# Seven products for one more pair in the output projection, its operand in eight forms, and the second weight sum written over the raw page

## The chip, the cores and the metric

The kernel runs on one core of a Trainium2 chip. The metric is the device time of one execution in microseconds (us). Engines are named as the profile names them: PE (TensorE matmuls), PEld (its weight loads), DVE (VectorE), ACT (ScalarE), POOL (GpSimd) and SP (SyncE, which here only issues DMAs).

## The reference, cut to what matters

Two layers, each with two large products; the change touches how both are computed, the second one most:

```python
for l in range(DEPTH):                      # 2 layers, SEQ = 256, D_MODEL = 4096
    h = rmsnorm(x, norm_w[l])
    proj = h @ w_in[l]                      # 4096 x 11264
    ...                                     # grouped attention and two-way retention on parts of proj
    x = x + jnp.concatenate([a_out, r_out], axis=-1) @ w_out[l]   # 4096 x 4096
return rmsnorm(x, final_norm)
```

All is in float32, so each product of the reference is made from high and low parts.

## The kernel before, in words

**Stages and blocks.** There are four stages: w_in and w_out of layer 0, then of layer 1. A w_in stage has 11 blocks, a w_out stage 4; a block makes 1,024 columns of the output for all 256 rows. Within a block the 4,096 rows of the weight are taken as 16 pairs of 128 + 128 rows. The activations are the stationary operand; the weights stream, 512 columns at a time.

**High and low parts.** A weight page arrives raw from HBM on SP's queue (`wraw`, 128x1024 float32, 512 KB). ACT rounds it to a high part (`whi`), DVE subtracts to get the low part (`wlo`). Operands are split in the same way. Each product is three matmuls of 128x512: high by high, high by low (both at line 1683), and low by high (line 1693).

**Eight products or seven.** A pair is a 2x2 by 2x2 block product. Plainly it takes eight products: two raw pages, 24 matmuls, operand `x8h`/`x8l` of four forms. The pairs in `SEVENS` (2, 5, 8, 9, 11, 13, in every stage) take seven products in Winograd's form: 21 matmuls, operand `x7h`/`x7l` of seven forms (A11, A12, S4, A22, S1, S2, S3). Their weights come as page A (raw), page T (`wv`: ACT copies the raw page, and a DMA from POOL's queue adds a second matrix to it, line 729), half a page B (`third`, 256 KB, split into `bhi`/`blo`) and page U (`wu`: two DVE sums of `wraw`, `wv` and `third`).

**Buffers.** There are 6 raw pages, 5 `whi`, 4 `wlo`, 2 `wv`, one `wu`. `Weights.begin` handles a page. At page T of a seven it makes the two sums into `wu` and calls `empty`, which frees the raw page and issues the next raw load. An eight's raw page is freed after its low part.

**What sets the order.** Nothing is scheduled on the chip: while the program is being written, a planner (`tick`, `room`, `low_parts`, `add_up`) keeps estimated clocks of ACT and DVE and decides where in each engine's fixed order a cast, a sum, a combine or a task of attention stands. Its constants are set per block by `assume(n)` from `PLANS`; `LOW_AHEAD` says how far ahead of PE's clock DVE may be given low parts.

**First blocks and block ends.** The first block of a stage (`opening`) takes its pairs in `FIRST_ORDER`, since its operands are only then being split (`split_pair`). At a block's end the last pair's products are sorted by PSUM bank, and `combine` adds the banks M1 to M8 into two result pages `ca` and `cb`: on DVE from the bank, or through an ACT copy (`out`) when DVE has more than `RELIEF` us queued. The next block starts in banks M3 and M8.

Of the kernel before, what the change touches and what calls it, by code (L numbers as in the profile page):

```python
# [12 lines left out]
F32R = mybir.dt.float32r  # L13
# [4 lines left out]
P = 128  # L18
# [19 lines left out]
A_EARLY = 0  # L38
# [36 lines left out]
SUM_SLACK = 0.3  # L75
# [24 lines left out]
LOW_AHEAD = 1.5  # L100
# [11 lines left out]
    1: {'LOW_AHEAD': 5.0},  # L112
    6: {'TIGHT_A': 8},
    7: {'SUM_SLACK': 0.0, 'AT_ONCE': 1, 'STRICT': 4},
    8: {'TIGHT_B': 5, 'STRICT': 5},
    9: {'THIRD_SLACK': 1.0, 'BANK_REST': 1.5, 'LOW_AHEAD': 1.0, 'RAW_SLACK': 1.0, 'RELIEF': 0.7, 'PASS': 0.1},
    14: {'STRICT': 9, 'TIGHT_A': 0},
    15: {'S_FIXED': 0.16, 'LONG': 2, 'EARLY': 1.8, 'PASS': 0.3, 'PE_REST': 2.0, 'NEAR': 30},
    22: {'PASS': 0.3, 'U_SLACK': 1.0, 'AT_ONCE': 1},
    24: {'V_FIXED': 0.12, 'TIGHT_B': 20, 'TIGHT_A': 2},  # L120
# [12 lines left out]
EIGHTS = [_p for _p in range(NP) if _p not in EVER]  # L133

# [110 lines left out]
LEADS = [8 * next(_i for _i, _p in enumerate(_o) if _p in SEVENS[_s]) for _s, _o in enumerate(FIRST_ORDER)]  # L245
# [91 lines left out]
def hybrid_encoder(  # L337
# [143 lines left out]
    class Weights:  # L481


        def __init__(self):
            self.pages, self.sevens = [], []
            for l in range(DEPTH):
                for w, twice, n in ((w_in, twice_in, N_IN), (w_out, twice_out, N_OUT2)):
                    for b in range(n):
                        stage = 2 * l + (w is w_out)
                        start = (l, b) == (0, 0) and w is w_in  # L490
                        for g in GROUPS[stage] if b else FIRST_GROUPS[stage]:
                            for slot in slots_of(g, stage, start):
# [3 lines left out]
                                one.seven = one.pair in SEVENS[stage] and not one.whole  # L496
# [139 lines left out]
        def begin(self, g):  # L636
# [12 lines left out]
            elif g.kind == PAGE_T:  # L649
# [4 lines left out]
                u = o.u = t(wp, [P, 2, NB], "wu", 1)  # L654
# [4 lines left out]
                self.empty(next(v for v in self.seq if v.own is o))  # L659
# [94 lines left out]
    def dead_room():  # L754

        if not rooms:
            e, o = len(EIGHTS), len(EVER)
# [6 lines left out]
            for p in range(NP):  # L764
                if p not in EIGHTS:
# [22 lines left out]

    def split_pair(p, v, whole, stage):
# [15 lines left out]
        if p in SEVENS[stage]:  # L805
# [20 lines left out]
            ve.tensor_sub(lo[:, 2:7, :], f, f32(hi)[:, 2:7, :])  # L826
            sums_of.pop()
            drop()
        else:
# [3 lines left out]
            else:  # L833
                both = [t(ap, [P, 7, P], v, len(EVER), F32R) for v in ("x7h", "x7l")]
                hi, lo = (v[:, 0:4, :].rearrange("p (i m) t -> p i (m t)", m=MT) for v in both)
# [1260 lines left out]
```

## Time and profile before

| | |
|---|---|
| median of 3 runs | 2599.41 us (2598.05 to 2601.19) |
| the profiled execution | 2599.34 us, its span 2597.6 us |
| PE busy | 2581.8 us, 99% of the span, 11,560 matmuls |
| PEld busy | 2135.2 us, 82% |
| DVE busy | 2215.3 us, 85% |
| ACT busy | 1853.6 us, 71% |
| DMA | 653.5 MB, mean 252 GB/s |
| PE clock | 0.998 of full speed over the span |

Busy time is the union of an engine's instructions. A 128x512 matmul is shown with 0.39 us from start to end, but the next one starts 0.23 us later, so that a pause of PE shows as idle only where it is longer than the overlap of 0.16 us.

### The profile page before, as it was taken

To read this page: it belongs to the slowest core of one execution; us is meant where nothing else is said; L and a number is where in the kernel's file an instruction comes from. 1 tells how busy PE (TensorE), PEld (TensorE's weight loads), DVE (VectorE), ACT (ScalarE), POOL (GpSimd) and SP (SyncE) were. 2 spreads that over 40 slices of the span, in tenths; PEclk is the share of its full clock that TensorE was granted. 3 is DMA by queue.
4 is the path that set the end of the run, shared out by engine and by line. 5 is a ranking of instruction groups with operands and counts; after the bars stand their busy time and mean duration, and the time that the engine had idled before them with its cause. 6 is when DMAs were issued, how large, how long until landed. Compare 5 with 4: busy or idle time off the path is not lost.

```text
span 2597.6 us, 34368 instructions
## 1 busy us (share of the span) xinstructions
PE 2581.8 (99%) x11560; PEld 2135.2 (82%) x11560; DVE 2215.3 (85%) x2710; ACT 1853.6 (71%) x2626; POOL 398.6 (15%) x548
## 2 busy tenths in 40 slices
PE   9999999999999999999999999999999999999998
PEld 7888888888888888888878888888888888888886
DVE  7898888888789898777979888889888798987777
ACT  8877777766666788656887667776666667886655
POOL 0111221221102100211111112221201021000000
PEclk9999999999999999999999999999999999999999
DMA  9988988888778778988888879888887787788886
GB/s 314 305 237 277 289 242 254 281 247 263 221 220 260 230 235 227 271 269 248 275 253 261 250 239 279 246 270 268 259 257 222 208 259 242 220 229 251 250 243 194
DMA packets 206594, 653.52 MB, mean 252 GB/s; under 512 B 24784, under 2 KB 31440, under 8 KB 206416
## 3 DMA queue, kind: packets, MB, share of 16 engines
q1 hardware_dynamic: 147040, 472.99, 51.8%
q0 software_dynamic: 58656, 177.24, 30.7%
q8 instruction: 90, 1.47, 0.2%
q10 hardware_dynamic: 720, 1.10, 0.1%
q14 instruction: 88, 0.72, 0.1%
HBM read 607.19 MB, written 44.04 MB: 251 GB/s over the span
## 4 chain that ended last, share of the span: by engine, by line
PE 94%; DMA 2%; DVE 2%; ACT 1%; issue 1%; SPq 0%; DVEq 0%; POOLq 0%; POOL 0%; ACTq 0%
PE M L1683 60%; PE M L1693 30%; PE M L1158 1%; PE M L1157 1%; PE M L1156 1%; DMA ca<-in_x 1%; DVE wlo L321 1%; ACT whi L321 1%; DMA third<-in_w_out 0%; PE M L1677 0%; DMA wraw<-in_w_out 0%; DVE cb L321 0%; DMA whole<-in_w_in 0%; ACT ca L321 0%; DVE ca L321 0%
## 5 line engine op out<-in xcount | busy, mean ns | idle before, releaser
L321 DVE TENSOR_TENSOR wlo<-wraw,whi 128x1024 fp32r<-128x1024 f32 (+1 forms) x774 | 935.3, 1215 | 172.8 <-issue 61.2
L321 ACT CAST whi<-wraw 128x1024 fp32r<-128x1024 f32 (+1 forms) x776 | 800.1, 1045 | 297.1 <-PE M L1683 283.0
L1683 PE MATMUL M<-whi,x8h 128*128 128x512 f32 x2368 | 922.5, 390 | 1.0 <-DVE cb L321 0.8
L1683 PE MATMUL M<-whi,x8l 128*128 128x512 f32 x2368 | 921.8, 389 | 0.0
L1693 PE MATMUL M<-wlo,x8h 128*128 128x512 f32 x2364 | 676.3, 389 | 0.2 <-DVE wlo L321 0.2
L1683 PEld LDWEIGHTS M<-whi,x8h 128*128 128x128 f32 x2368 | 444.6, 188 | 94.9 <-DVE cb L321 1.5
L1683 PEld LDWEIGHTS M<-whi,x8l 128*128 128x128 f32 x2368 | 444.6, 188 | 92.4 <-DVE x8l L321 0.3
L1693 PEld LDWEIGHTS M<-wlo,x8h 128*128 128x128 f32 x2364 | 442.2, 188 | 91.4 <-DVE wlo L321 1.0
L1683 PE MATMUL M<-whi,x7h 128*128 128x512 f32 x1080 | 420.5, 389 | 0.2 <-ACT whi L321 0.2
L1683 PE MATMUL M<-whi,x7l 128*128 128x512 f32 x1080 | 420.3, 389 | 0.0
L1693 PE MATMUL M<-wlo,x7h 128*128 128x512 f32 x1080 | 334.4, 390 | 0.7 <-DVE wlo L321 0.6
L729 POOL DMA_DIRECT2D wv<-in_twice_in x132 | 118.5, 898 | 1068.6 <-ACT wv L321 923.8
L321 ACT CAST whi<-wu 128x1024 fp32r<-128x1024 f32 x180 | 189.3, 1052 | 91.9 <-DVE wu L321 54.2
L321 ACT CAST whi<-wv 128x1024 fp32r<-128x1024 f32 x180 | 189.0, 1050 | 91.5 <-PE M L1683 51.9
L321 DVE TENSOR_TENSOR wlo<-wv,whi 128x1024 fp32r<-128x1024 f32 x180 | 219.6, 1220 | 37.3 <-PE M L1693 30.7
L321 ACT COPY wv<-wraw 128x1024 f32<-128x1024 f32 x180 | 188.9, 1049 | 74.7 <-DMA wraw<-in_w_out 35.2
L321 DVE TENSOR_TENSOR wlo<-wu,whi 128x1024 fp32r<-128x1024 f32 x180 | 219.1, 1217 | 24.8 <-PE M L1693 16.7
L1693 PEld LDWEIGHTS M<-wlo,x7h 128*128 128x128 f32 x1080 | 202.4, 188 | 44.1 <-DVE wlo L321 2.5
L1683 PEld LDWEIGHTS M<-whi,x7h 128*128 128x128 f32 x1080 | 202.8, 188 | 42.6 <-ACT whi L321 0.9
L1683 PEld LDWEIGHTS M<-whi,x7l 128*128 128x128 f32 x1080 | 202.8, 188 | 41.8
L321 DVE TENSOR_TENSOR wu<-wu,third 128x512 f32<-128x512 f32 x180 | 124.6, 692 | 7.0 <-DMA third<-in_w_in 0.8
L321 DVE TENSOR_TENSOR wu<-wraw,wv 128x512 f32<-128x512 f32 x180 | 123.1, 684 | 8.7 <-DMA wv<-in_twice_in 6.3
(249 smaller groups left out, 2292.0 us busy)
## 6 DMA issues: line engine op xcount, KB each, us to landing
wraw<-in_w_in SPq DMA_DIRECT2D x568, 512.0 KB, 5.2
wraw<-in_w_out SPq DMA_DIRECT2D x208, 512.0 KB, 5.4
wv<-in_twice_in POOLq DMA_DIRECT2D x132, 512.0 KB, 7.5
third<-in_w_in SPq DMA_DIRECT2D x132, 256.0 KB, 5.8
wv<-in_twice_out POOLq DMA_DIRECT2D x48, 512.0 KB, 8.1
third<-in_w_out SPq DMA_DIRECT2D x48, 256.0 KB, 5.7
full<-next_dram POOLq DMA_DIRECT2D x18, 512.0 KB, 9.5
p_dram<-room POOLq DMA_DIRECT2D x64, 128.0 KB, 3.4
```

The costliest lines, as they stand in the source:

```text
L321: return call(out, *args, **kwargs)
L729: self.adds.pop(0)[1]()
L1156: nc.tensor.matmul(out, a[0], b[0], start=start, stop=False)
L1157: nc.tensor.matmul(out, a[0], b[1], start=False, stop=False)
L1158: nc.tensor.matmul(out, a[1], b[0], start=False, stop=stop)
L1683: nc.tensor.matmul(acc[name], a[i], g.hi[h], start=m == first[name] and not i, stop=False)
L1693: nc.tensor.matmul(acc[name], a, g.lo[h], start=False, stop=m == final[name])
```

## The change

- Pair 3 joins `SEVENS` in the two w_out stages (`FLEX = (3,)`). In the first block of such a stage it still takes eight products (`OPENING` leaves it out); in the other three blocks seven.
- Its operand has eight forms (`xfh`/`xfl`, 128x8x128): the seven of before and A21, so that both ways find what they need. In the w_in stages four of them hold the plain operand.
- The second sums are made in place: `u = o.a`, the raw page. `wu` is gone, and the raw page is freed after the low part of page U instead of after the sums.
- `A_EARLY` 1 moves the load of each seven's raw page one place earlier; `SUM_SLACK` is 0.0, `LOW_AHEAD` 3.0; `PLANS` and three of the four `SPREAD`s have other values.

```diff
-A_EARLY = 0
+A_EARLY = 1
-SUM_SLACK = 0.3
+SUM_SLACK = 0.0
-LOW_AHEAD = 1.5
+LOW_AHEAD = 3.0
 PLANS = {
...
-    15: {'S_FIXED': 0.16, 'LONG': 2, 'EARLY': 1.8, 'PASS': 0.3, 'PE_REST': 2.0, 'NEAR': 30},
+    15: {'AT_ONCE': 2, 'SUM_SLACK': 0.0, 'V_FIXED': 0.14, 'PE_REST': 1.5, 'U_SLACK': 0.3, 'RUSH': 2.0},
...
-SEVENS = ((2, 5, 8, 9, 11, 13), (2, 5, 8, 9, 11, 13), (2, 5, 8, 9, 11, 13), (2, 5, 8, 9, 11, 13))
+SEVENS = ((2, 5, 8, 9, 11, 13), (2, 3, 5, 8, 9, 11, 13), (2, 5, 8, 9, 11, 13), (2, 3, 5, 8, 9, 11, 13))
+FLEX = (3,)
+OPENING = tuple(tuple(_p for _p in _s if _p not in FLEX) for _s in SEVENS)
...
-SPREAD2 = (2, 3, 6, 7, 10, 13)
+SPREAD2 = (3, 4, 6, 9, 13, 14)
...
-                u = o.u = t(wp, [P, 2, NB], "wu", 1)
+                u = o.u = o.a
                 ve.tensor_add(u[:, 0, :], o.a[:, 1, :], o.v[:, 0, :])
                 ve.tensor_add(u[:, 1, :], u[:, 0, :], o.b)
-                self.empty(next(v for v in self.seq if v.own is o))
...
-                self.parts(g, o.u)
+                self.parts(g, o.u, then=partial(self.empty, next(v for v in self.seq if v.own is o)))
...
+            n = 8 if p in FLEX else 7
+            hi, lo = seven_room(p)
+            f = page([P, n - 2, P], "xf")
             ac.copy(a22, x1[:, 1])
+            if p in FLEX:
+                ac.copy(tokens(f)[:, 5], x1[:, 0])
...
-            ac.copy(hi[:, 2:7, :], f)
+            ac.copy(hi[:, 2:n, :], f)
...
+            elif p in SEVENS[stage]:
+                a = at(operand[p], ALL, {(0, 0): A11, (1, 0): A12, (1, 1): A22, (0, 1): 7}[index], ALL)
```

PE, second w_out block of layer 0, the first of pair 3's two pages, before (`x8h_8540` is pair 3's operand; M1 to M8 are the banks):

```order
L1683 MATMUL M3_9609<-whi_9699,x8h_8540 128x512
L1683 MATMUL M3_9609<-whi_9699,x8l_8541 128x512
L1683 MATMUL M8_9616<-whi_9699,x8h_8540 128x512
L1683 MATMUL M8_9616<-whi_9699,x8l_8541 128x512
L1683 MATMUL M4_9633<-whi_9699,x8h_8540 128x512
L1683 MATMUL M4_9633<-whi_9699,x8l_8541 128x512
L1683 MATMUL M2_9636<-whi_9699,x8h_8540 128x512
L1683 MATMUL M2_9636<-whi_9699,x8l_8541 128x512
L1693 MATMUL M3_9609<-wlo_9719,x8h_8540 128x512
L1693 MATMUL M8_9616<-wlo_9719,x8h_8540 128x512
L1693 MATMUL M4_9633<-wlo_9719,x8h_8540 128x512
L1693 MATMUL M2_9636<-wlo_9719,x8h_8540 128x512
```

The second page has twelve more of the same. Of the change, in the same place, the last two pages of pair 3, B and U (`xfh_8376` is its operand):

```order
L1697 MATMUL M2_9568<-bhi_9667,xfh_8376 128x512
L1697 MATMUL M2_9568<-bhi_9667,xfl_8377 128x512
L1707 MATMUL M2_9568<-blo_9668,xfh_8376 128x512
L1697 MATMUL M6_9670<-whi_9684,xfh_8376 128x512
L1697 MATMUL M6_9670<-whi_9684,xfl_8377 128x512
L1697 MATMUL M4_9565<-whi_9684,xfh_8376 128x512
L1697 MATMUL M4_9565<-whi_9684,xfl_8377 128x512
L1707 MATMUL M6_9670<-wlo_9701,xfh_8376 128x512
L1707 MATMUL M4_9565<-wlo_9701,xfh_8376 128x512
```

Pages A and T have six each, so that pair 3 now has 21 matmuls for 24; over the whole program PE's order has 11,547 rows where it had 11,565.

DVE in the same stretch, before (rows 2 and 4 are the low parts of pair 3's two pages, row 6 the low part of pair 2's page U):

```order
L321 TENSOR_TENSOR wlo_9701<-wraw5_9555,whi_9677 128x1024
L321 TENSOR_TENSOR wlo_9719<-wraw4_9586,whi_9699 128x1024
L321 STREAM_TRANSPOSE room_9711<-ca_9530 128x1024
L321 TENSOR_TENSOR wlo_9747<-wraw3_9614,whi_9715 128x1024
L321 STREAM_TRANSPOSE room_9737<-cb_9531 128x1024
L321 TENSOR_TENSOR wlo_9773<-wu_9661,whi_9742 128x1024
```

And with the change:

```order
L325 TENSOR_TENSOR wlo_9630<-wraw5_9434,whi_9610 128x1024
L325 TENSOR_TENSOR wraw5_9434<-wraw5_9434,wv_9516 128x512
L325 TENSOR_TENSOR wraw5_9434<-wraw5_9434,third_9514 128x512
L325 TENSOR_TENSOR wlo_9646<-wraw3_9478,whi_9628 128x1024
L325 STREAM_TRANSPOSE room_9638<-ca_9459 128x1024
L325 TENSOR_TENSOR wlo_9662<-wv_9516,whi_9644 128x1024
L325 TENSOR_TENSOR wlo_9686<-wraw4_9537,whi_9660 128x1024
L325 TENSOR_TENSOR blo_9668<-third_9514,bhi_9667 128x512
L325 STREAM_TRANSPOSE room_9680<-cb_9460 128x1024
L325 TENSOR_TENSOR wlo_9701<-wraw5_9434,whi_9684 128x1024
```

Pair 3 now has four low parts and two sums on DVE where it had two low parts, and its raw page `wraw5_9434` is held from its first row here to its last.

DVE at the end of the first block of layer 1, before (`M3_11784` and `M8_11791` are that block's banks; `wlo` rows belong to the block that follows):

```order
L321 SCALAR_TENSOR_TENSOR cb_12433<-cb_12433,M5_11903 128x512
L321 TENSOR_TENSOR cb_12433<-cb_12433,M3_11784 128x512
L321 TENSOR_TENSOR wlo_12517<-wraw5_12385,whi_12481 128x1024
L321 TENSOR_TENSOR cb_12433<-cb_12433,M8_11791 128x512
L321 TENSOR_TENSOR ca_12432<-ca_12432,M4_11820 128x512
```

And with the change:

```order
L325 SCALAR_TENSOR_TENSOR cb_12402<-cb_12402,M5_11887 128x512
L325 TENSOR_TENSOR wlo_12444<-wraw5_12281,whi_12416 128x1024
L325 TENSOR_TENSOR cb_12402<-cb_12402,out_12451 128x512
L325 TENSOR_TENSOR cb_12402<-cb_12402,out_12464 128x512
L325 TENSOR_TENSOR ca_12401<-ca_12401,M4_11735 128x512
```

There banks M3 and M8 are now emptied by ACT copies (`out`), and DVE adds the copies instead of the banks; a low part stands ahead of both.

## Rows read from the trace of the kernel before

**Rows 1.** The page: span, and busy time of each engine.

```profile
span 2597.6 us, 34368 instructions
PE 2581.8 (99%) x11560; PEld 2135.2 (82%) x11560; DVE 2215.3 (85%) x2710; ACT 1853.6 (71%) x2626; POOL 398.6 (15%) x548
```

**Rows 2.** Waits of PE: engine, line, releaser: us in total, times, longest.

```profile
PE M L1693 <- DVE wlo L321: 0.8, 2, 0.6
PE M L1683 <- DVE cb L321: 0.8, 1, 0.8
PE M L1683 <- DVE ca L321: 0.2, 1, 0.2
PE M L1683 <- ACT whi L321: 0.2, 1, 0.2
```

**Rows 3.** Busy time in stretches: the last three w_out blocks of each layer.

```profile
core 0: us, PE busy (x) PEld busy (x) DVE busy (x) ACT busy (x) POOL busy (x), PEclk, DMA share, GB/s
1037.00:1285.00 248.00, 248.00 (x1095) 205.33 (x1095) 200.08 (x228) 167.22 (x222) 43.27 (x60) 1.00 0.88 271
2325.00:2572.00 247.00, 246.39 (x1087) 203.63 (x1086) 194.07 (x209) 156.06 (x187) 20.91 (x24) 1.00 0.82 241
```

**Rows 4.** Busy time in stretches: the two stretches in which a w_out stage opens.

```profile
900.00:1000.00 100.00, 100.00 (x459) 83.46 (x459) 91.54 (x133) 83.86 (x134) 8.70 (x11) 1.00 0.77 229
2200.00:2300.00 100.00, 100.00 (x458) 83.14 (x457) 91.54 (x130) 85.14 (x136) 10.16 (x11) 1.00 0.77 229
```

**Rows 5.** Timeline of PE, rows with idle time in brackets: start, us, instruction.

```profile
1290.83 0.50 PE L1693 MATMUL M<-wlo,x8h 128*128 128x512 f32 x1 [0.22 <-DVE wlo L321]
...
1298.41 0.50 PE L1683 MATMUL M<-whi,x8h 128*128 128x512 f32 x1 [0.23 <-DVE ca L321]
...
1332.88 0.50 PE L1683 MATMUL M<-whi,x7h 128*128 128x512 f32 x1 [0.17 <-ACT whi L321]
...
1382.15 0.50 PE L1683 MATMUL M<-whi,x8h 128*128 128x512 f32 x1 [0.80 <-DVE cb L321]
...
2571.36 0.50 PE L1693 MATMUL M<-wlo,x7h 128*128 128x512 f32 x1 [0.61 <-DVE wlo L321]
```

**Rows 6.** Timeline of DVE and of ACT at the end of layer 1's first block.

```profile
1380.28 1.22 DVE L321 TENSOR_TENSOR wlo<-wraw,whi 128x1024 fp32r<-128x1024 f32 x1
1381.41 0.68 DVE L321 TENSOR_TENSOR cb<-cb,M 128x512 f32<-128x512 f32 x1
...
1380.03 2.00 ACT L321 CAST whi<-wraw 128x1024 fp32r<-128x1024 f32 x2 [2.06 <-PE M L1683]
```

**Rows 7.** Groups by line and form: xcount | busy us, mean ns | idle before.

```profile
L321 DVE TENSOR_TENSOR wlo<-wraw,whi 128x1024 fp32r<-128x1024 f32 x768 | 931.3, 1219 | 172.8 <-issue 61.2 <-ACT whi L321 51.1 <-PE M L1693 48.4
L321 DVE TENSOR_TENSOR blo<-third,bhi 128x512 fp32r<-128x512 f32 x180 | 123.1, 684 | 0.0
L321 DVE TENSOR_TENSOR wu<-wraw,wv 128x512 f32<-128x512 f32 x180 | 123.1, 684 | 8.7 <-DMA wv<-in_twice_in 6.3
L321 ACT CAST whi<-wraw 128x1024 fp32r<-128x1024 f32 x768 | 795.3, 1050 | 295.4 <-PE M L1683 281.3 <-ACT whi L321 4.6 <-issue 4.6
L321 ACT CAST bhi<-third 128x512 fp32r<-128x512 f32 x180 | 111.2, 618 | 15.1 <-PE M L1683 14.5 <-DMA third<-in_w_in 0.4
L321 DVE TENSOR_TENSOR x7l<-xf,x7h 128x640 fp32r<-128x640 f32 x24 | 19.7, 819 | 3.7 <-ACT x7h L321 3.7
L321 DVE TENSOR_TENSOR x8l<-full,x8h 128x256 fp32r<-128x256 f32 x42 | 15.8, 417 | 0.6 <-ACT x8h L321 0.6
L321 DVE TENSOR_TENSOR xf<-xf,full 128x128 f32<-128x128 f32 x21 | 6.0, 285 | 1.8 <-ACT xf L321 1.5
```

**Rows 8.** Raw pages: SP's waits before their loads, their landing, and one wait of DVE.

```profile
SPq L531 <- DVE wu L321: 606.3, 175, 9.0
...
DMA to landing us min/median/max: 3.0/5.3/14.9
...
DVE wlo L321 <- PE M L1693: 95.8, 122, 1.6
```

More of the change, by code (lines that the diff above doesn't have):

```diff
@@ L216 @@
 ]
-SPREAD = (3, 5, 8, 11, 12, 13)
+SPREAD = (3, 5, 8, 10, 12, 13)
 SPREAD1 = (4, 7, 8, 10, 12, 14)
-SPREAD2 = (2, 3, 6, 7, 10, 13)
-SPREAD3 = (6, 7, 9, 11, 12, 14)
+SPREAD2 = (3, 4, 6, 9, 13, 14)
+SPREAD3 = (5, 7, 9, 12, 13, 14)
 def opening_order(stage):
     spread = (SPREAD, SPREAD1, SPREAD2, SPREAD3)[stage]
-    spread = spread if len(spread) == len(SEVENS[stage]) else SEVENS[stage]
-    order = [_p for _p in ([1, 0] if stage == 0 else [0, 1]) + list(range(2, NP)) if _p not in SEVENS[stage]]
-    for i, p in zip(spread, SEVENS[stage]):
+    spread = spread if len(spread) == len(OPENING[stage]) else OPENING[stage]
+    order = [_p for _p in ([1, 0] if stage == 0 else [0, 1]) + list(range(2, NP)) if _p not in OPENING[stage]]
+    for i, p in zip(spread, OPENING[stage]):
         order.insert(i, p)
@@ L236, in grouped @@
     for p in order:
-        if p in SEVENS[stage] or not groups:
+        if p in OPENING[stage] or not groups:
             groups.append(())
@@ L244, with pages_of @@
 FIRST_GROUPS = [grouped(_o, _i) for _i, _o in enumerate(FIRST_ORDER)]
-LEADS = [8 * next(_i for _i, _p in enumerate(_o) if _p in SEVENS[_s]) for _s, _o in enumerate(FIRST_ORDER)]
+LEADS = [8 * next(_i for _i, _p in enumerate(_o) if _p in OPENING[_s]) for _s, _o in enumerate(FIRST_ORDER)]
 SHARED = ("M1", "M5", "M7", "M6")
-def pages_of(group, stage, first=False):
-    n = 1 if group[0] in SEVENS[stage] else 0
+def pages_of(group, sevens, first=False):
+    n = 1 if group[0] in sevens else 0
     order, one, rest = [], group[:n], group[n:]
@@ L262, in pages_of, with slots_of @@
     return order + rest
-def slots_of(group, stage, first=False):
-    for _p, _k in pages_of(group, stage, first):
-        if _p in SEVENS[stage] and not (first and _p in NATIVE):
+def slots_of(group, sevens, first=False):
+    for _p, _k in pages_of(group, sevens, first):
+        if _p in sevens and not (first and _p in NATIVE):
             yield [(_b, _p, (ALL, _a), _k, _h) for _b, _a, _pg, _h in SEVEN_PRODUCTS if _pg == _k]
@@ L490, in __init__ @@
                         start = (l, b) == (0, 0) and w is w_in
+                        sevens = SEVENS[stage] if b else OPENING[stage]
                         for g in GROUPS[stage] if b else FIRST_GROUPS[stage]:
-                            for slot in slots_of(g, stage, start):
+                            for slot in slots_of(g, sevens, start):
                                 one = Page()
@@ L495, in __init__ @@
                                 one.whole = start and one.pair in NATIVE
-                                one.seven = one.pair in SEVENS[stage] and not one.whole
+                                one.seven = one.pair in sevens and not one.whole
                                 one.begun, one.low_at, one.empty, one.raw_at = False, None, False, 1e9
@@ L833, in split_pair @@
             else:
[L834 to L835 removed]
+                hi, lo = (v[:, 0:4, :].rearrange("p (i m) t -> p i (m t)", m=MT) for v in seven_room(p))
             if whole is None:
@@ L1552, in block @@
         rush[0] = RUSH if hurried else 0.0
+        sevens = OPENING[stage] if opening else SEVENS[stage]
         for g in FIRST_GROUPS[stage] if opening else GROUPS[stage]:
-            for slot in slots_of(g, stage, first_order):
+            for slot in slots_of(g, sevens, first_order):
                 flat += slot
```

32 lines of the change are left out of this document (17 added, 15 removed).

## The prediction, made before the changed kernel was run

> **What bounds the kernel now.** I read the page first: PE is busy for 2581.8 us of a span of 2597.6 us, DVE for 85% and ACT for 71% of it [rows 1]. Busy PE alone proves little, because the records of neighbouring matmuls overlap, so the second view is the count of matmuls in a stretch without pauses: the last three w_out blocks of layer 0 hold 1095 matmuls in 248.00 us, which is 0.2265 us each, at the full granted clock of 1.00 [rows 3]. Those three blocks need 3 x 366 = 1098 matmuls (10 pairs of 24, 6 of 21), so there is no hole in them: PE takes its next matmul as soon as it can, and the time of such a block is its number of matmuls. The third view is what PE waited for: wlo 0.8, cb 0.8, ca 0.2 and whi 0.2 us, 2.0 us in all the steady work [rows 2]. The timeline puts these at five places, four where layer 0 goes over into layer 1 and one near the end [rows 5]. Each hides 0.16 us more under the overlap (0.39 us shown, 0.23 us apart), so these five pauses are worth 0.22 + 0.23 + 0.17 + 0.80 + 0.61 + 5 x 0.16 = 2.83 us. That is all that better order could win here; the rest is matmuls, the start and the tail.
>
> The Trainium skill speaks against this reading. Its page "Perfetto Trace Analysis", section "Identifying the Most-Contended Engine", says that busy time of matmuls is no good measure for TensorE, that the busy share of weight loads should be taken instead, and that the most-contended engine is the one with the highest occupancy. By that PE stands at 82% and DVE at 85%, and DVE would be the bound; the second rival below is what that would mean. The count of matmuls in a stretch disagrees with it here.
>
> **Part by part.** *Removed matmuls.* Pair 3 goes from 24 to 21 matmuls in three w_out blocks of each of two layers: 6 x 3 = 18 fewer, which is also the difference of PE's two orders. On the path, since PE has no hole there: 18 x 0.2265 = 4.08 us less.
>
> *Added casts, low parts and sums.* As eight products, pair 3 needs two low parts on DVE (2 x 1.22 = 2.44 us) and two casts on ACT (2 x 1.05 = 2.10). As seven it needs three whole low parts, a half one and two sums: 3 x 1.22 + 0.68 + 2 x 0.68 = 5.70 us on DVE; and three casts, a half one and a copy, 4 x 1.05 + 0.62 = 4.82 us, on ACT, where I take the copy for a cast of its size [rows 7]. That is 3.26 us of DVE and 2.72 us of ACT more per block, 19.6 and 16.3 us in six blocks. In the stretch of layer 0, DVE works 200 of 248 us and ACT 167; with three such blocks this becomes 210 and 175 of 247, and in layer 1 less [rows 3]. PE stays the fullest by 37 us per three blocks, so I cost it at nothing. What hides it is the lead of DVE over PE: it waited 122 times for PE to give a low page back [rows 8], so all four low pages were full then. If that cover were gone, all 19.6 us would show.
>
> *The operand in eight forms.* In each opening of w_out pair 3's split grows. DVE: from two low parts of 256 (0.83 us) to four sums of 0.29, one low part of 256 and one of 768: 1.14 + 0.42 + 0.82 x 768/640 = 2.54 us, an estimate from those rows; so 1.7 us more per layer [rows 7], and something over 1 us on ACT. The two stretches where this falls show DVE at 91.54 of 100 us and PE without idle [rows 4]: 8.5 us are free for 1.7. Bounds: nothing, or 3.4 us in both layers. I take 0.5 us, near the lower end, because the free time is five times the need, but the work comes in bursts.
>
> *The raw page held longer.* This concerns all 180 sevens. Before, SP waited 175 times for the sums into `wu` (606.3 us) and then issued the next raw load [rows 8]; now that load stands behind the low part of page U, one or more low parts later in DVE's order, and behind the waiting load on SP's queue stand later raw loads and the thirds. In the orders I counted, for each raw load, the matmuls from PE's use of the low part that frees the page (or the one next after the sums) to the first matmul on the new page: never under 58 before; 37 once in nearly every block now, and 19 at one place. 37 matmuls are 37 x 0.2265 = 8.4 us; a landing takes 5.3 us in the middle and the cast 1.05 us [rows 7, 8], 6.4 us, so 2.0 us are left even if DVE had no lead. The worst landing of 14.9 us would not be covered. For the sevens themselves, whose added matrix needs the raw page earliest, `A_EARLY` makes up for it: from the freeing low part to page T's first matmul I count at least 76 matmuls, 72 before. Bounds: nothing, or 0.5 us in each of 30 blocks. I take nothing.
>
> *One stall goes.* The longest wait of PE, 0.80 + 0.16 = 0.96 us at 1382.15, is for bank M8: DVE did a low part of 1.22 us first and added the bank only from 1381.41 to 1382.09, while ACT sat idle for 2.06 us [rows 5, 6]. In the changed order both M3 and M8 are emptied there by ACT copies, which need no turn on DVE. I take 0.96 us off. What is late next is not PE's bank but the added copy, which nobody on PE waits for.
>
> *Other order.* At ten block ends of attention and retention a low part that PE uses 16 matmuls (3.6 us) or more after the bank now stands ahead of M3's add, which was so nowhere before. M3 is wanted 19 matmuls, 4.3 us, after its last product, and M8, with 15, stood behind such a low part before in seven of these ends without an idle row; so nothing, and up to 0.4 us each, 4 us, if DVE comes late. The other four pauses, 2.83 - 0.96 = 1.87 us, I leave as they are: ahead of three of them DVE's two orders carry a like amount of work, and the fourth, ACT's, I can't tell. Added DMA is 256 KB in each of six blocks, 1.5 of 653 MB: nothing.
>
> Sum, against the profiled execution of 2599.34 us: - 4.08 - 0.96 + 0.5 = - 4.54, giving 2594.8 us. The median of the three runs is 2599.41, so the same offset holds: 2594.8 us, 0.18% less.
>
> **Rivals.** *The last pauses close as well.* The change has other numbers for the block that opens layer 1, where four of the five pauses lie. If they all go and the openings cost nothing: 2599.4 - 4.08 - 2.83 = 2592.5 us. For it: that block's order is wholly different. Against it: low parts and combines are as many as before.
>
> *DVE is the bound.* Then the removed matmuls win nothing and the 19.6 + 3.4 = 23.0 us added to DVE show: 2599.4 + 23.0 = 2622 us. For it: 85% over the span, 91.5% in the openings [rows 1, 4]. Against it: not one missing matmul in the last three blocks and DVE itself waiting for PE [rows 3, 8]. This is the result that the rule cited above would give (the Trainium skill, "Perfetto Trace Analysis", "Identifying the Most-Contended Engine").
>
> *Raw pages run short.* The rival on the slower side: with six raw pages, each seven's held until page U's low part is made, the load of the eight that follows the pairs 8 and 9 comes late in every block. It decides from the point where landing and cast take more than 8.4 us plus DVE's lead. At 0.5 us in each of 30 blocks: 2594.8 + 15 = 2609.8 us. For it: landings of up to 14.9 us. Against it: the middle one leaves 2.0 us, and no cast of a raw page is among PE's longer waits now [rows 2].
>
> *New bursts eat the gain.* The eighth form's work in the openings at its full 3.4 us, or late M3 banks at ten block ends: 2594.8 + 3 to 4 = about 2598.5 us, inside no change.
>
> *The change doesn't do what it says*: the orders show the 18 matmuls gone, so this has no weight of its own.
>
> **How the numbers follow.** A measurement of this kernel can tell about 0.2%, 5.2 us, from no change; faster means under 2594.2, slower over 2604.6. Chances: the forecast 0.50, spread from 2593.3 to 2597 (0.17 of it under 2594.2); all pauses close 0.18; the gain is eaten 0.22; raw pages 0.09, of which 0.03 stay under 2604.6; DVE 0.01. So faster 0.35, same 0.33 + 0.22 + 0.03 = 0.58, slower 0.07. The range leaves out half of the raw-page case, DVE, and the ends beyond both sides: 2591.3 to 2600.5 us.
>
> **What would show it.** Right: PE 11,542 matmuls; the last three w_out blocks of a layer 9 matmuls or 2.0 us shorter each time, without idle; DVE near 2238 us; no wait of PE for cb at the end of layer 1's first block. Wrong: waits of PE for `whi` with ACT waiting for raw pages once per block (raw pages); waits for `wlo` between the second and fifth pair of the last three w_out blocks (DVE); waits for cb or ca just after block ends (late banks); or pauses in the openings, near 900 to 960 and 2200 to 2250 us.

## The result, and the profile after

The changed kernel takes 2607.28 us (2605.61 to 2608.99), the kernel before beside it 2599.26 us: a ratio of 1.0032 [1.0022, 1.0041], slower by 8 us where 4.5 us less were predicted. The page of the changed kernel, span and busy time of each engine:

```profile
span 2607.1 us, 34396 instructions
PE 2580.5 (99%) x11542; PEld 2132.5 (82%) x11542; DVE 2241.7 (86%) x2742; ACT 1874.5 (72%) x2657; POOL 402.6 (15%) x554
```

Against [rows 1], the 18 matmuls are gone, DVE works 26 us more and ACT 21. PE is busy 1.3 us less, but the span is 9.5 us longer, so PE stands still more. Busy time in stretches that lie in the last three w_out blocks of each layer, to be set beside [rows 3]:

```profile
core 0: us, PE busy (x) PEld busy (x) DVE busy (x) ACT busy (x) POOL busy (x), PEclk, DMA share, GB/s
1037.00:1283.00 246.00, 245.86 (x1085) 203.23 (x1084) 205.87 (x231) 170.59 (x216) 45.95 (x63) 1.00 0.92 276
2331.00:2576.00 245.00, 244.82 (x1081) 202.45 (x1080) 204.23 (x221) 167.85 (x202) 23.50 (x27) 1.00 0.88 253
```

There next to nothing went wrong: 0.2267 us for each matmul, at the full clock, with 0.14 and 0.18 us of idle time. What PE waited for in the steady work (columns as in [rows 2]):

```profile
PE M L1697 <- DVE ca L325: 3.0, 3, 1.7
PE M L1697 <- ACT x8h L325: 2.9, 1, 2.9
PE M L1707 <- DVE wlo L325: 2.9, 4, 1.5
PE M L1697 <- ACT whi L325: 2.2, 2, 1.1
PE M L1707 <- DVE blo L325: 0.8, 1, 0.8
PE M L1697 <- ACT bhi L325: 0.7, 1, 0.7
```

That is 12.5 us where [rows 2] has 2.0. The timeline puts nearly all of it into first blocks of a stage and the block ends ahead of them (start, us, instruction, idle time ahead of it and what ended it):

```profile
75.02 0.73 PE L1707 MATMUL M<-wlo,x7h 128*128 128x512 f32 x2 [0.65 <-DVE wlo L325]
76.49 0.50 PE L1697 MATMUL M<-bhi,x7h 128*128 128x512 f32 x1 [0.73 <-ACT bhi L325]
78.02 0.51 PE L1707 MATMUL M<-blo,x7h 128*128 128x512 f32 x1 [0.80 <-DVE blo L325]
...
895.34 0.47 PE L1697 MATMUL M<-whi,x7h 128*128 128x512 f32 x1 [1.74 <-DVE ca L325]
...
915.17 0.50 PE L1697 MATMUL M<-whi,x8h 128*128 128x512 f32 x1 [1.11 <-ACT whi L325]
...
1326.88 1.21 PE L1707 MATMUL M<-wlo,x8h 128*128 128x512 f32 x4 [1.45 <-DVE wlo L325]
...
1368.45 0.49 PE L1697 MATMUL M<-whi,x8h 128*128 128x512 f32 x1 [2.93 <-ACT x8h L325]
...
2208.45 0.50 PE L1697 MATMUL M<-whi,x8h 128*128 128x512 f32 x1 [1.11 <-ACT whi L325]
```

**One sum holds for all kernels of this study.** I took the starts of all matmuls from 20 us on and added up what lies over 0.2267 us between two of them (0.1176 us for 256 columns), wherever it is over 0.06 us too much. These pauses, slow matmuls behind a pause included, are 5.0 us in the kernel before and 18.9 us in the changed one. The time of a profiled execution less its pauses is 2594.0 to 2594.7 us in all nine kernels with 11,560 matmuls, and 2589.6 to 2590.6 in all eleven with 11,542. So the removed matmuls are worth about 4.2 us everywhere, as costed, and everything else that these kernels differ by is pauses of PE. The sum says where the time lies, not why. In the table the median and its ratio, to the kernel before as timed beside each, come from all runs, the pauses from the one profiled execution:

| kernel | median us | ratio to before | pauses us |
|---|---|---|---|
| before | 2599.26 | | 5.0 |
| changed | 2607.28 | 1.0032 [1.0022, 1.0041] | 18.9 |
| e1_old_numbers | 2653.83 | 1.0211 [1.0196, 1.0226] | 61.7 |
| e2_new_numbers | 2617.36 | 1.0071 [1.0054, 1.0088] | 23.5 |
| e3_in_place | 2641.44 | 1.0164 [1.0149, 1.0179] | 46.9 |
| e4_no_pair3 | 2624.64 | 1.0095 [1.0080, 1.0110] | 30.5 |
| e5_early_0 | 2638.51 | 1.0156 [1.0141, 1.0171] | 47.8 |
| e6_seven_raws | 2620.61 | 1.0085 [1.0070, 1.0100] | 26.3 |
| e7_nudge_before | 2619.13 | 1.0080 [1.0065, 1.0095] | 27.7 |
| e8_nudge_after | 2613.45 | 1.0052 [1.0035, 1.0068] | 23.6 |
| e9_in_place_early | 2624.90 | 1.0100 [1.0086, 1.0113] | 32.4 |
| e10_small_nudge | 2600.62 | 1.0006 [0.9997, 1.0015] | 6.4 |
| e11_same_order | 2596.92 | 0.9993 [0.9984, 1.0002] | 6.3 |
| e12_block_15 | 2610.03 | 1.0042 [1.0029, 1.0056] | 19.4 |
| e13_refit_after | 2605.44 | 1.0023 [1.0014, 1.0032] | 15.1 |
| e14_refit_before | 2599.17 | 1.0000 [0.9991, 1.0009] | 4.6 |
| e15_refit_less | 2605.01 | 1.0026 [1.0015, 1.0038] | 12.6 |
| e16_early_not_0 | 2603.95 | 1.0018 [1.0009, 1.0027] | 14.2 |
| e17_early_not_0_15 | 2605.14 | 1.0021 [1.0011, 1.0030] | 15.5 |
| e18_refit_early_not_0 | 2601.94 | 1.0011 [1.0002, 1.0020] | 12.9 |

**Where the changed kernel's pauses begin.** ACT works through its instructions in the program's order, and at three places it waits some 3 us for weights. The timeline of ACT around 61, 888 and 1324 us, and then around 914:

```profile
64.65 1.05 ACT L325 CAST whi<-wraw 128x1024 fp32r<-128x1024 f32 x1 [3.17 <-DMA wraw<-in_w_in]
...
888.64 1.05 ACT L325 COPY wv<-wraw 128x1024 f32<-128x1024 f32 x1 [2.88 <-DMA wraw<-in_w_in]
...
1316.07 0.63 ACT L325 ACTIVATE room<-ca 128x512 f32<-128x512 f32 x1 [1.45 <-DMA ca<-in_x]
...
1318.26 1.04 ACT L325 COPY wv<-wraw 128x1024 f32<-128x1024 f32 x1
1319.21 1.99 ACT L325 CAST whi<-wraw 128x1024 fp32r<-128x1024 f32 x2
1324.26 1.05 ACT L325 CAST whi<-wv 128x1024 fp32r<-128x1024 f32 x1 [3.06 <-DMA wv<-in_twice_in]
```

```profile
906.52 3.31 ACT L325 COPY ca<-room 32x256 f32<-32x256 f32 x8 [3.22 <-DVE room L325]
...
912.41 1.65 ACT L325 COPY ca<-room 32x256 f32<-32x256 f32 x4
914.08 1.04 ACT L325 CAST whi<-wraw 128x1024 fp32r<-128x1024 f32 x1
```

The first two are waits for a raw page: behind them come the pauses at 74 to 78 us (3.0 us in all) and the late bank at 895 (2.0 us). But the second is no work of the change. The kernel before has it too, and no pause behind it:

```profile
884.81 1.05 ACT L321 COPY wv<-wraw 128x1024 f32<-128x1024 f32 x1 [3.42 <-DMA wraw<-in_w_in]
...
898.68 1.65 ACT L321 COPY ca<-room 32x256 f32<-32x256 f32 x4 [1.68 <-DVE room L321]
```

So at 895 it is not the wait that is new, but what stands behind it: after that wait the changed order has one more cast on ACT, and four small subtractions on DVE, ahead of the add that gives PE its bank back. The third wait is of another kind: the raw page was there, but its copy into `wv` stands only three instructions ahead of the cast that wants it back with the second matrix added, and behind a wait for the residual. Behind it come the low part at 1326 (1.7 us) and the late operand `x8h` of the last pair: 5.1 us, 3.1 of waiting and 2.0 in slow matmuls after it. From 1325 to 1369 us ACT has a single idle moment of 0.29 us, so nothing there makes up for that wait; but ACT also does more in that stretch, 34.1 of the 35 us from 1330 to 1365 where the kernel before has 31.0, and which of the two makes `x8h` late is not shown. The pauses at these three places make 11.8 of the 18.9 us. At 914 and 2207 (1.4 us each) ACT has waited 3.2 us for a page that DVE turns, for 1.7 and 2.0 in the kernel before, and makes eight and then four copies out of it ahead of the cast that PE needs.

### The profile page after: what moved, and what is told of

Read it like the earlier page. It is cut to its first block, busy times and chain, and to the rows that moved or that the text cites. A ratio compares the mean times of both kernels' runs of the same rounds, so it can differ in the third digit from the quotient of the medians.

```text
span 2607.1 us, 34396 instructions
## 1 busy us (share of the span) xinstructions
PE 2580.5 (99%) x11542; PEld 2132.5 (82%) x11542; DVE 2241.7 (86%) x2742; ACT 1874.5 (72%) x2657; POOL 402.6 (15%) x554
## 5 line engine op out<-in xcount | busy, mean ns | idle before, releaser
L325 DVE TENSOR_TENSOR wlo<-wraw,whi 128x1024 fp32r<-128x1024 f32 x954 | 1150.0, 1215 | 188.2 <-PE M L1707 61.2
L325 ACT CAST whi<-wraw 128x1024 fp32r<-128x1024 f32 x956 | 983.0, 1046 | 359.9 <-PE M L1697 249.2
L1697 PE MATMUL M<-whi,x8h 128*128 128x512 f32 x2128 | 829.5, 390 | 5.6 <-ACT x8h L325 2.9
L1697 PE MATMUL M<-whi,x8l 128*128 128x512 f32 x2128 | 829.1, 390 | 0.0
L1707 PE MATMUL M<-wlo,x8h 128*128 128x512 f32 x2124 | 611.9, 390 | 1.5 <-DVE wlo L325 1.5
L1697 PEld LDWEIGHTS M<-whi,x8h 128*128 128x128 f32 x2128 | 399.9, 188 | 90.7 <-ACT x8h L325 3.3
L325 DVE TENSOR_TENSOR wraw<-wraw,wv 128x512 f32<-128x512 f32 x186 | 128.0, 688 | 13.3 <-DMA wv<-in_twice_in 7.1
L325 DVE TENSOR_TENSOR wraw<-wraw,third 128x512 f32<-128x512 f32 x186 | 128.7, 692 | 7.5 <-DMA third<-in_w_in 1.1
L325 ACT CAST bhi<-third 128x512 fp32r<-128x512 f32 x186 | 114.9, 618 | 18.2 <-PE M L1697 17.4
L325 DVE TENSOR_TENSOR blo<-third,bhi 128x512 fp32r<-128x512 f32 x186 | 127.3, 684 | 0.0
```

The costliest lines, as they stand in the source:

```text
L325: return call(out, *args, **kwargs)
L1697: nc.tensor.matmul(acc[name], a[i], g.hi[h], start=m == first[name] and not i, stop=False)
L1707: nc.tensor.matmul(acc[name], a, g.lo[h], start=False, stop=m == final[name])
```

## The experiments

Two theories at first, with others in the texts: **raw pages** (holding a raw page until page U's low part is what costs) and **numbers** or, from the fifth run on, **fit** (the order that the planner writes is only as good as its numbers were chosen for just this structure).

**e1 to e4: which part of the change costs.**

```diff
e1, the changed kernel:     A_EARLY 0, SUM_SLACK 0.3, LOW_AHEAD 1.5, PLANS and SPREADs of before
e2, the kernel before:      A_EARLY 1, SUM_SLACK 0.0, LOW_AHEAD 3.0, PLANS and SPREADs of the change
e3, the kernel before:
-                u = o.u = t(wp, [P, 2, NB], "wu", 1)
-                self.empty(next(v for v in self.seq if v.own is o))
+                u = o.u = o.a
-                self.parts(g, o.u)
+                self.parts(g, o.u, then=partial(self.empty, next(v for v in self.seq if v.own is o)))
e4, the changed kernel:     pair 3 takes eight products everywhere, its operand four forms
```

> The changed kernel (pair 3 as seven, eight forms, sums over the raw page) with the planner's numbers of the kernel before: A_EARLY 0, SUM_SLACK 0.3, LOW_AHEAD 1.5, its PLANS and its SPREADs. In the changed kernel's trace PE's pauses beyond the period of its matmuls add up to some 19 us (5 before), all of them where stages open or end. Raw pages (the page held longer makes loads late, which makes ACT wait at its copies and PE after it): this has nothing to do with the numbers, so 2603 to 2609 us with the pauses at the same kinds of place. Numbers (the retuned constants alone give an order that pauses): pauses back to about 5 us, 2594 to 2597 us. Split of eight forms (more work per opening of w_out): only the pauses near 890 to 915 and 2187 to 2208 us stay, 2600 to 2602 us.

> The kernel before with the new planner's numbers alone (A_EARLY 1, SUM_SLACK 0.0, LOW_AHEAD 3.0, new PLANS and SPREADs); separate sums and six sevens as before. Numbers: pauses of 15 us or more, 2607 to 2613 us. Raw pages, and split of eight forms: 2597 to 2601 us, as before.

> The kernel before with one edit: the second sums over the raw page, which is freed after page U's low part; numbers and pairs as before. Raw pages: slower, 2604 to 2612 us, with ACT waiting for raw pages at its casts (it never did before) and PE after it. Numbers, and split of eight forms: 2597 to 2601 us.

> The changed kernel without pair 3: the sums over the raw page and the new numbers, pair 3 at eight products everywhere with a plain operand. Raw pages or numbers: as the changed kernel with its 18 matmuls back, 2609 to 2613 us. Split of eight forms: without the pauses near 890 to 915 and 2187 to 2208 us (5.8 us in all), so 2604 to 2606 us, and those pauses gone from the trace.

In e1 and e3 the gates of attention groups 2 and 3 of layer 0 are stored over those of groups 0 and 1 before these are fetched, so that two groups are multiplied by other gates; the amount of work is the same. Measured: 2653.83, 2617.36, 2641.44 and 2624.64 us. Every mixture is slower than either whole kernel. The sums in place cost 42 us with the old numbers; the new numbers cost 18 us on the old structure, and on the new one they win 47 (e1 to the change). Pair 3 with everything around it is 17 us faster than without it. None of the theories foresaw this, and effects that simply add up cannot give it: 42 and 18 us would make 60, and e4, which has both, is 25 us slower than the kernel before. Nor is e3 the held page alone. Its order is a new one too: about 1,470 of the 2,710 instructions of DVE in the trace stand in another place, where in e7 (below), counted the same way, it is some 400.

e4 also bears on the eight forms, though its order is another one. Without them it still has 4.5 us of pauses where the w_out stages open (at 896, 916, 2201 and 2221 us), for 5.8 us in the changed kernel: most of those pauses need no eighth form.

**e5, e9 and e6: the raw pages by themselves.** e5 is the changed kernel, e9 the kernel e3, and e6 the kernel e4, each with one number changed.

```diff
e5:
-A_EARLY = 1
+A_EARLY = 0
e9:
-A_EARLY = 0
+A_EARLY = 1
e6:
-RAWS = 6
+RAWS = 7
```

> The changed kernel with A_EARLY back at 0 and nothing else: the raw page of a seven is loaded one place later again. Raw pages (holding the raw page until page U's low part is what costs, and the earlier load is what pays most of it back): ACT waits for the added matrix (wv<-in_twice) rise from 22 + 15 us towards the 66 + 36 us of the kernel with all the old numbers, and the time is at least 2630 us. Fit (each order written by the planner is only as good as its numbers were tried for it, and any other order costs 5 to 20 us, whatever it is): 2612 to 2627 us, with pauses at the openings and no such rise of one wait.

> The kernel before with the sums in place (2641.4 us by itself) and A_EARLY 1, its other numbers left as they were. Raw pages (what the sums in place cost by themselves is the late load of a seven's raw page, and A_EARLY 1 takes that back): ACT's waits for the added matrix fall from 59 us at wv<-in_twice_in to below 30, and the time by 15 to 30 us, to 2612 to 2627: the 20 us over the kernel before that the nudged one showed stay. Fit alone: A_EARLY is one more untried number, the time stays within 10 us of 2641.

> The changed kernel without pair 3 (which took 2624.6 us) with seven raw pages for six; the room is that of the wu page, which is free there. Raw pages: ACT's waits for raw pages (20.1 + 5.4 us at whi, 23.9 + 21.0 at wv) fall to less than a third, PE's waits for whi (5.6 us) go, and the time falls by 10 to 20 us, to 2605 to 2615. Fit: ACT waits less there, but the time stays within 10 us of 2624.6, on either side, since the order is again one that no number was tried for.

Measured: 2638.51 us without the earlier load (31 us more), 2624.90 us with it (16.5 us less than e3), 2620.61 us with a seventh page (4 us less). ACT's waits in e5, then in e9 (us in total, times, longest):

```profile
ACT whi L325 <- DMA wv<-in_twice_in: 59.4, 30, 9.3
ACT wv L325 <- DMA wraw<-in_w_in: 51.5, 32, 5.3
ACT whi L325 <- DMA wv<-in_twice_out: 48.8, 16, 7.1
```

```profile
ACT wv L321 <- DMA wraw<-in_w_in: 41.3, 23, 5.0
ACT whi L321 <- DMA wraw<-in_w_in: 23.3, 13, 5.0
ACT wv L321 <- DMA wraw<-in_w_out: 23.1, 15, 2.8
ACT whi L321 <- DMA wv<-in_twice_in: 13.1, 9, 3.1
```

With A_EARLY 0 a seven's added matrix comes late, thirty times and up to 9.3 us in e5; over w_in and w_out ACT's waits for it are 108.2 us there for 37.2 in the changed kernel. With A_EARLY 1 the first of these waits falls from 58.9 us (e3) to 13.1 (e9), and a wait for raw pages at casts takes its place, 32.5 us, which the kernel before does not have. That second wait comes with the earlier loads, at least in part: e2, where no page is held longer, has 15.7 us of it. So the raw page held longer does cost when its load is left where it was, and the earlier load pays a part back. How much is the page alone is not shown, since each of these runs has another order as well: another order of the changed kernel costs 6 us (e8, below) for e5's 31, but in e7 a new order with no page held longer raises the same wait for the added matrix from 18.5 to 39.4 us. A seventh page takes ACT's waits for the added matrix from 29.1 to 6.0 us, those for raw pages at casts from 25.5 to 1.9 and PE's for `whi` from 5.6 to 1.9, but the time falls by 4 us, not the 10 to 20 expected: other pauses came in their place, as fit had it.

**e7, e8 and e10: another order of the same work.**

```diff
e7 (before) and e8 (changed):
-S_FIXED = 0.2
+S_FIXED = 0.205
e10 (before):
-PE_REST = 1.5
+PE_REST = 1.52
```

> The kernel before with one estimate of the planner, ACT's fixed cost of an instruction (S_FIXED), at 0.205 for 0.2 us: the same work, with some 700 of 2556 rows of DVE's order and 480 of 2008 of ACT's in another place. Raw pages: nothing about pages has changed, 2597 to 2603 us. Fit: 5 to 20 us slower, 2604 to 2620, in pauses at openings and where layer 0 goes over into layer 1.

> The changed kernel with the same nudge, S_FIXED 0.205 for 0.2: the same work, with some 960 of 2590 rows of DVE's order and 375 of 2041 of ACT's in another place. Raw pages: 2604 to 2611 us. Fit: 5 to 20 us slower, 2612 to 2627; if the changed kernel's numbers were tried less than those of before, it may as well come out a few us faster.

> The kernel before with another estimate of the planner nudged, PE_REST 1.52 for 1.5 us: the same work, with 70 of 2556 rows of DVE's order and 84 of 2008 of ACT's in another place, a tenth of the rows that the first nudge moved. Fit: a cost by the places where it moves rows, so less than the 20.3 us of the first nudge: 2600 to 2612 us. If an order is only as good as the whole of it was tried, even this costs 15 us or more.

Measured: 2619.13, 2613.45 and 2600.62 us. An estimate that is 0.005 us off its tuned value, with no work added or removed, costs the kernel before 20 us and the changed one 6; a nudge that moves a tenth of the rows costs at most 4 us (the interval ends at 1.0015). PE's waits in e7, to be set beside [rows 2]:

```profile
PE M L1156 <- ACT ca L321: 3.5, 2, 3.1
PE M L1683 <- DVE D L321: 2.6, 2, 1.9
PE M L1683 <- ACT x8h L321: 2.6, 2, 2.1
PE M L1693 <- DVE wlo L321: 2.4, 5, 1.0
PE M L1683 <- DVE x8l L321: 2.1, 1, 2.1
PE M L1683 <- DVE cb L321: 1.3, 3, 0.9
```

They are spread over whatever comes to stand badly. The fit theory holds, for these three orders; raw pages alone would have had e7 and e8 unchanged. How much another order costs depends on the order, from nothing that shows to 20 us.

**e11: the gain without the new order.** TensorE of the kernel before leaves out three low products of pair 3 per block.

```diff
+                if p == 3 and stage % 2 and not opening and k == PAGE_B and m != final[name] and cut[0] < 3:
+                    cut[0] += 1
+                else:
                     nc.tensor.matmul(acc[name], a, g.lo[h], start=False, stop=m == final[name])
```

> The kernel before with every order as it was, in which TensorE leaves out 18 matmuls: three low products of pair 3 in each of the last three output blocks of both layers, so that part of the low parts of pair 3 is missing from the output. This is the gain of the change without its new order. If PE has no hole there, as the prediction has it, 18 x 0.2265 = 4.08 us go: 2595.2 us. If another engine sets the pace of these blocks, nothing goes: 2599.3 us.

Measured: 2596.92 us, 2.0 us less, with an interval from 4 us less to half a us more. In its last three blocks of layer 0:

```profile
1037.00:1283.00 246.00, 246.00 (x1087) 203.75 (x1086) 198.95 (x228) 166.54 (x222) 43.31 (x60) 1.00 0.89 273
```

The 4.08 us are there in the sum (2590.3 us without pauses for 2594.3), but 1.3 us come back as pauses in the profiled execution; that PE now catches up with the other engines sooner is my reading of it. So the gain that the change is about is at most 4 us, and in the medians not clear of nothing.

**e12: the numbers of before in the block that opens layer 1.**

```diff
-    15: {'AT_ONCE': 2, 'SUM_SLACK': 0.0, 'V_FIXED': 0.14, 'PE_REST': 1.5, 'U_SLACK': 0.3, 'RUSH': 2.0},
+    15: {'S_FIXED': 0.16, 'LONG': 2, 'EARLY': 1.8, 'PASS': 0.3, 'PE_REST': 2.0, 'NEAR': 30},
```

> The changed kernel with the numbers of before in one block alone, the one that opens layer 1 (PLANS[15]): 21 rows of DVE's order and 23 of ACT's stand in another place, all between 1290 and 1400 us, where four of its pauses lie (1.7 us at 1325, 3.1 + 2.0 at 1365). Fit: the result is changed by that stretch alone, by what its pauses become: between 2600.5 us (both go) and 2612 (they grow to the 7.3 + 2.8 us that the kernel without pair 3 has there). The turns of the new operand stand earlier on ACT in it, so I expect 2600 to 2605. Raw pages: nothing about pages has changed, 2607.

Measured: 2610.03 us. My 2600 to 2605 was wrong: the pauses of that stretch moved to 1332, 1338, 1367 and 1382 us and make 8.7 us for 6.8. In this block, numbers that served one structure don't serve the other. In the same profile the bank at 893 costs 3.7 us for 2.0, with every order the same up to there: the pause itself is 0.2 us longer, and 1.5 us are slow matmuls behind it, which the changed kernel does not have there. So what a pause costs varies by a microsecond or two from one execution to the next.

**e13 to e15: numbers chosen anew.**

```diff
e13, the changed kernel (e15 is without the changes in 2, 15 and the SPREADs but the 3 in SPREAD1, and has 'STEP_V': 1.5 in 25):
+    1: 'V_FIXED': 0.12      2: 'LONG': 3      9: 'LOW_AHEAD': 1.0      10: 'EARLY': 1.8
+    11: 'AT_ONCE': 1, 'PE_REST': 1.0, no LOW_AHEAD      12: 'NEAR': 20      15: 'ADD_SLACK': 0.3
+    25: 'S_FIXED': 0.18      26: 'V_FIXED': 0.14
+SPREAD1 = (3, 7, 9, 10, 12, 14)
+SPREAD3 = (5, 7, 9, 10, 13, 14)
e14, the kernel before:
+    0: 'LONG': 3      14: 'PASS': 0.3      25: 'LOW_AHEAD': 2.0      26: 'PASS': 0.2
+SPREAD1 = (4, 7, 8, 10, 12, 13)
```

> The changed kernel with other numbers for nine blocks (1, 2, 9 to 12, 15, 25, 26) and one place in two of the SPREADs; the work is the same, 254 of 2590 rows of DVE's order and 268 of 2041 of ACT's move, nearly all in openings and where attention and retention end. Structure (raw pages held longer and more work in the openings make the pauses): the pauses stay at 15 to 25 us, 2604 to 2614 us. Fit: the pauses at 893, 914, 1325, 1365, 2187 and 2207 us (11 us of 18.9) shrink by most of their size, 2594 to 2601 us.

> The kernel before with other numbers, chosen with the same effort, in four blocks (0, 14, 25, 26) and one place of a SPREAD. Its pauses are 5.0 us in all, so that no more than that can go: fit has 2596 to 2600 us, within 3 us of the kernel before; if the order is worth nothing by itself, 2599.

> As the refitted changed kernel, with the numbers of fewer blocks (1, 9 to 12, 25, 26) and one place of a SPREAD: block 15, which opens layer 1, has the changed kernel's own numbers again. Structure: 2604 to 2614 us. Fit: the pauses at 893, 914, 2187 and 2207 us (5.9 us of 18.9) go and those of layer 1's opening (6.8 us) stay at least in part: 2596 to 2604 us.

Measured: 2605.44, 2599.17 and 2605.01 us. Both forms of the change lie in the range of the structure theory, not in that of fit. The pauses at 181, 893, 914, 2207 and 2578 us, 7.1 us, are gone in e13 but for 0.8, and only 2 us of that reach the median: the pauses at 74 us and in the opening of layer 1 (7.5) stay. At 74 us they are the same three in the same order as in the changed kernel, which has 3.0 us there; in e13's profiled execution slow matmuls behind them make it 5.9. Where the bank was late at 895, ACT of e13 and e15 still waits for the raw page (3.3 and 2.4 us); ahead of 914 it waits only 1.7 us for the turned page, and at 2207 in e13 ACT's instructions are the same, but the turned page comes 1.1 us sooner against PE's matmuls. PE's waits in e15:

```profile
PE M L1701 <- ACT x8h L329: 2.8, 1, 2.8
PE M L1711 <- DVE wlo L329: 2.4, 3, 1.6
PE M L1711 <- DVE blo L329: 0.8, 1, 0.8
PE M L1701 <- ACT bhi L329: 0.7, 1, 0.7
```

No late bank is left. Most of what is left (nearly 11 of 12.6 us) stands behind the same two waits of ACT as in the changed kernel; in e15:

```profile
64.61 1.05 ACT L329 CAST whi<-wraw 128x1024 fp32r<-128x1024 f32 x1 [3.12 <-DMA wraw<-in_w_in]
...
1319.76 1.05 ACT L329 CAST whi<-wv 128x1024 fp32r<-128x1024 f32 x1 [3.04 <-DMA wv<-in_twice_in]
```

So fit is right for a part of the pauses, and a like search on the kernel before (e14) found nothing to take. Against the kernel before, the refitted change still takes 6 us more.

**e16 to e18: A_EARLY undone in opening blocks alone.** e16 and e17 start from e15, e18 from e13.

```diff
-                if g.seven and i > RAWS + A_EARLY:
+                if g.seven and i >= 26:
e17:
+                if g.seven and i >= 26 and not 387 <= i < 413:
```

> The refitted changed kernel with fewer numbers (2605.0 us), with A_EARLY undone in block 0 alone: the raw pages of the sevens in the first 26 loads come in their plain order. 6 rows of DVE's order and 29 of ACT's move. Raw pages: ACT's wait of 3.1 us at 61 us goes and with it the pauses of 3.0 us at 74, and the later ones stay: 2601 to 2603 us. Fit: the pauses at 74 us stay or move by some us within that block, 2603 to 2608.

> As the run with A_EARLY undone in block 0, and undone in block 15 too, which opens layer 1. There ACT waits 3.0 us for the added matrix of a seven ahead of the pauses, and without A_EARLY that seven's raw page comes later still. Raw pages: the pauses of layer 1's opening (1.9 + 6.0 us) grow, 2 to 6 us slower than the run with block 0 alone. Fit: within 3 us of it, on either side.

> The refitted changed kernel (2605.4 us) with A_EARLY undone in block 0 alone. Raw pages: its pauses of 3 to 6 us at 74 us go, 2599.5 to 2602.5 us, level with the kernel before; those of layer 1's opening (7.5 us) stay. Fit: 2603 to 2608.

Measured: 2603.95, 2605.14 and 2601.94 us. ACT around 61 us in e16, where the changed kernel has its wait of 3.17 us:

```profile
60.51 1.05 ACT L329 COPY wv<-wraw 128x1024 f32<-128x1024 f32 x1 [0.28 <-DMA wraw<-in_w_in]
62.21 1.05 ACT L329 CAST whi<-wv 128x1024 fp32r<-128x1024 f32 x1 [0.65 <-DMA wv<-in_twice_in]
```

The wait shrinks (in e18 to 1.68 us), and the pauses behind it with it, from 3.0 us in e15 to 1.8 in e16 and from 5.9 in e13 to 2.6 in e18, not to nothing; 2.9 of e13's 5.9 us were slow matmuls. Of the time 1.1 us go in e16, which the spread of its runs does not tell from nothing, and 3.5 in e18. So at 61 us it is the order of raw loads that A_EARLY changed. e18 came out where raw pages had it, e16 where fit had it. In layer 1's opening undoing A_EARLY makes no difference that shows (e17 is 1.2 us slower than e16, within what fit had); my reading is that the copy into `wv` is late there, not the page. e18 is the fastest form of the change, and still 0.11% [0.02, 0.20] behind the kernel before. What stays open is layer 1's opening, 8 to 9 us of pauses in e15 to e18 where the kernel before has 3.8: no order that closes it on this structure was found.

## Why the prediction was wrong, point by point

- **18 matmuls, 4.08 us: right.** 11,542 matmuls, the three last w_out blocks all but without a hole, 4.2 us in the sum over all kernels. With the order kept (e11) 2.0 us of it, 4 to nothing by the interval, reach the median.
- **Casts, low parts and sums cost nothing: right.** DVE works 2241.7 us (2238 predicted) and in the last three blocks of layer 0 206 of 246 us, where PE stands idle for 0.14. That DVE is the bound was wrong. The Trainium skill ("Perfetto Trace Analysis", "Identifying the Most-Contended Engine") takes the highest occupancy for the most-contended engine, with the share of weight loads as one of two measures for TensorE; the other, the share of peak arithmetic, was not worked out here. By the weight loads the trace does not agree: DVE with 86% stands above their 82%, and yet the 1085 matmuls of that stretch start 0.2267 us apart in the mean.
- **The stall at bank M8 goes: right.** No wait for `cb` is left. But the pauses of that stretch, 1290 to 1385 us, are 6.8 us for 3.8.
- **The raw page held longer costs nothing: wrong, by how much is open.** I bounded it by "nothing, or 0.5 us in each of 30 blocks", from a count of matmuls between the freeing low part and the use of the next page. In steady blocks that holds: 0.14 and 0.18 us of idle time in the two stretches above. But without the earlier load the changed kernel loses 31 us (e5). e3's 42 us are the held page and a new order together. In the changed kernel as it stands, the wait for a page at 61 us, with 3.0 us of pauses behind it, is the one that the kernel before does not have, and e16 and e18 put it down to the earlier loads, which were to make up for the held page. The sign that I gave for this rival, waits once per block, looked in the wrong place.
- **Openings, 0.5 us of at most 3.4: wrong.** The two openings of w_out have 5.8 us of pauses. I priced the added instructions against free time, 8.5 of 100 us [rows 4], but most of it needs no eighth form: e4, without it, has 4.5 us there. Nor is it enough that an engine waits 3 us, as ACT of the kernel before does at 884 us for nothing. It cost where what PE needed next stood behind that wait.
- **Other order, nothing or up to 4 us: the step that failed most.** I gave a price to ten block ends only and left the rest of the moved rows at nothing, since work was as before. The pauses rose from 5.0 to 18.9 us, where my sum had them fall by about half a us; 9.8 us of them, at 75 and from 1326 to 1373 us, lie where I had added nothing. e7 measures what I should have asked: one other order of the same work costs this kernel 20 us, against 5.0 us of pauses that its tuned order has. (Even these 5.0 I took for 2.83, since I counted only pauses that show as idle time.) The new numbers were a gain on the new structure (47 us over the old ones), but what they had to catch up with was an order already tried out block by block. With this price the forecast would have been no gain, with most of the chance on slower; I gave that 0.07. Why layer 1's opening pauses for 6.8 us is followed to a wait and a full queue on ACT, but stays open.

## What to carry to other kernels

When a kernel's order was written by a tuned planner, a change that moves many rows may start behind: nudge some of its numbers, work unchanged, and take the losses (here 20 us, 6 us, and at most 4 us for a nudge that moved few rows) as what the change may first have to earn back. A margin counted in steady blocks says little about a stage's opening: there follow a wait of an in-order queue to the end of what it delays, and look whether the kernel before has the same wait at no cost. And count the pauses from the matmuls' starts: if time less pauses is one constant for each number of matmuls, as here in twenty kernels, the time lies in the pauses, and what is left to ask is where they are and why.

## What the runs showed of the hardware

A pause of PE may cost more than its length. Busy time and granted clock in the two stretches with the pause of 2.93 us and behind it, in the changed kernel (columns as above):

```profile
1365.00:1369.00 4.00, 1.07 (x5) 0.35 (x3) 2.10 (x4) 4.00 (x9) 0.86 (x1) 1.00 0.85 205
1369.00:1373.00 4.00, 4.00 (x11) 3.17 (x12) 2.66 (x5) 1.81 (x5) 0.00 (x0) 0.57 1.06 273
```

Behind the pause the clock is granted at 0.57 in the mean of 4 us, that is mostly at its lower level of 1.2 GHz; seven matmuls start 0.43 us apart for 0.23, and with the slower starts beside them that adds 2.0 us to the 3.1 of the pause. In e7 a pause of 3.07 us is followed by a stretch at 0.50:

```profile
605.00:609.00 4.00, 0.93 (x4) 0.50 (x3) 3.37 (x4) 3.40 (x5) 0.00 (x0) 0.83 0.53 186
609.00:613.00 4.00, 4.00 (x10) 3.12 (x10) 4.00 (x9) 3.95 (x8) 0.00 (x0) 0.50 0.67 204
```

Behind the pauses of 1.74 us at 895 and 1.45 us at 1326 in the changed kernel the matmuls start 0.23 us apart again at once, or nearly. But the length of a pause does not decide it. In e3 one of 3.09 us, at 1363, is followed by the full clock, and in e13 three of 0.7 to 0.8 us, between 74 and 78 us, by 0.50, where the changed kernel has the same three, in the same order of instructions, and keeps the full clock. The stretch behind them in e3, e13 and the changed kernel (columns as above):

```profile
1363.00:1367.00 4.00, 3.77 (x16) 3.11 (x17) 3.93 (x6) 4.00 (x6) 0.00 (x0) 1.00 0.29 84
...
78.00:82.00 4.00, 4.00 (x10) 3.17 (x11) 3.97 (x6) 3.97 (x7) 0.00 (x0) 0.50 0.58 193
...
78.00:82.00 4.00, 3.98 (x17) 3.31 (x18) 3.97 (x5) 3.97 (x7) 0.00 (x0) 1.00 0.60 192
```

So a part of a kernel's time that looks like order is the clock: e13's profiled execution loses 2.9 us more than the changed kernel's at one and the same place.
